# Giving the attention an accumulator bank of its own beside the second input projection

## The chip, the cores and the metric

The kernel runs on one core of one Trainium2 chip. The metric is the device time of one execution in microseconds; lower is better. A core has a matrix engine (TensorE, in the profile PE), VectorE (DVE), ScalarE (ACT), GpSimd (POOL) and SyncE (SP), which start transfers or compute side by side, each in its own fixed order. TensorE writes its results into eight accumulator banks of 512 single-precision columns; VectorE and ScalarE read them out.

## The reference, cut to what matters

One encoder layer runs over two sequences of 16 learned and 256 given positions (272 in all, width 1024), with shared weights.

```
h    = layer_norm(concat([meta, x]))
proj = h @ w_in                                   # z | xbc | dt | c_q | c_kv | k_rope
xbc  = silu(depthwise_conv(proj[xbc], conv_w))    # 5 taps; then the state-space scan in both directions
y_ssm  = rms_norm((y_f + y_b + d_skip * xs) * silu(z))
q      = rms_norm(c_q) @ w_uq ;  k_nope, v = rms_norm(c_kv) @ w_ukv
o      = softmax((q_nope k_nope^T + q_rope k_rope^T) / sqrt(96)) v       # 8 heads
y_attn = rms_norm(o)
h = layer_norm(alpha * h + concat([y_ssm, y_attn]) @ w_out)
h = layer_norm(alpha * h + peer_ffn(h))           # 8 heads choose 16 of 16384 experts each
```

## The kernel before

**Stages.** The first sequence is projected (`win(0)`), with its attention (`mla(0)`) mixed in. Then the second is projected (`win(1)`), while the first one's state-space scan (`ssd(0)`) and the second one's attention (`mla(1)`) are mixed in. After that come the first sequence's output projection (`wout(0)`) and expert queries, with the rest of `mla(1)` and `ssd(1)`, and at last the expert layer, which takes most of the time. The order of the last part is written out by hand (`manual_schedule`). In everything ahead of it a planner places each engine's instructions from the order of the program and its own estimate of when each can run; the chip then runs each engine's list as placed, and an instruction that has to wait holds up all behind it.

**Banks.** Each of the eight banks is a tile with one buffer. A new tile in a bank must wait until the last reader of the tile before it is done. `BANKS` gives, stage by stage, the banks of five users: the attention's scores and other small products (`at()`), the scan (`sa()`), the projection (`pm()`), the output projection (`wa()`), and the attention's products with weights (`mp()`). `phase(n)` sets them; a user takes its banks in turn, and starts a new turn only where its set has changed. In the first stage the projection has banks 0 to 2 and `mp()` has bank 7. In the second both have 0, 1 and 2, each with a turn of its own. In the third the projection has none and `mp()` has bank 2; in the fourth the projection has 0 and 1.

**The projection.** `win(s)` runs over 18 blocks of 128 channels and, in between, over four gate units of two tiles each, 26 accumulator tiles in all, in the order `W1`: 12, 8, 13, 9, 14, 15, 16, 17, 10, z0, 11, 0, z1, 1, 2, z2, 3, 4, z3, 5, 6, 7. A tile takes 24 matmuls (8 pieces of the width, each as three products of high and low parts, line 174). Weights are split into `whi` and `wlo` on ScalarE and VectorE (lines 151, 152), two of each in flight. What empties a tile depends on the block. Blocks 0 to 11 take one pass on ScalarE (line 433) and four convolution passes on VectorE (line 436), and line 440 then works without the bank. A gate tile takes a tanh (line 415) and a product (line 417). Blocks 13 to 17, the low-rank inputs of the attention, take a copy into `cn` (line 450) and a square into `sq` (line 452). `cn` has one buffer, so the second sequence's copies wait for the first attention's last read of it; `sq` has three, so blocks 16 and 17 must wait for the sums over the first three squares (line 459), which sit in a score bank.

**The attention.** `mla(1)` first computes scales: `Rk` is the copy of line 340, at the end of a chain of sums, a Newton root (`nrq`) and a broadcast (line 338). Then come eight key products (lines 355 and 356: two matmuls into a bank, then a product with `Rk` on VectorE that empties it), six value products (lines 363 and 364), and for each head a query product (line 370), read out as `qT` (lines 372, 373). For each block of queries there follow scores (line 376), maximum and scale (378, 379), exponential `Pm` (382), transposes (385), a copy `PT` (387), and the product with the values (391). Line 167 multiplies the key, value and query products, and those of `W_out`.

```
    mix(w1, (sd0, RS), (mla1, RM1))
```

mixes per step of the projection 0.55 steps of the scan and 0.3 of the attention. The first key products come in the program behind the tiles of z0, and all key and value products before z1's second tile.

Of the kernel before, what the change touches and what calls it, by code (L numbers as in the profile page):

```python
# [46 lines left out]
EROWS, MRATE = 4, 0.8  # L47
HP = 400
RM, RS2, RM3, RS3, Q0 = 0.6, 0.6, 1.0, 0.7, 13
BANKS = (((3, 4, 5, 6), (), (0, 1, 2), (), (7,)), ((3, 4, 5), (6, 7), (0, 1, 2), (), (0, 1, 2)),  # L50
         ((3, 4, 5), (6, 7), (), (0, 1), (2,)), ((3, 4, 5), (6, 7), (0, 1), (), (2,)),
         ((3, 4), (6, 7), (2, 5), (0, 1), ()), ((3, 4, 5), (6, 7), (0, 1, 2), (), ()))
DEL = (3, 2)
# [9 lines left out]
def build(ctx, tc, i, o):  # L63
# [189 lines left out]
    def phase(n):  # L253
        for k, b in enumerate(BANKS[n]):
            if b != held.get(k):
                held[k] = b
                sets[k] = banks(*b)
# [1133 lines left out]
```

## Time and profile before

| | |
|---|---|
| median of 3 runs | 1744.48 us |
| lowest and highest | 1744.19 and 1745.67 us |
| the profiled execution, its own time | 1745.9 us |
| its span in the profile | 1743.9 us |
| TensorE busy | 1678.4 us (96%) |
| VectorE busy | 1384.8 us (79%) |
| ScalarE busy | 683.4 us (39%) |
| GpSimd busy | 427.9 us (25%) |
| mean granted clock of TensorE | 0.978 |

The profile is one execution. Its span is 2.0 us shorter than the time that was measured for it. Busy time is the time in which an engine had an instruction under way; times below count from the span's start. The granted clock is a share of TensorE's full clock.

### The profile page before, as it was taken

The page shows a single profiled execution, that of the slowest core. Times are in us where ns is not written, and L with a number is a line of the kernel's source. Part 1 is how long each engine was busy: PE and PEld are TensorE (multiplying, and loading weights), DVE is VectorE, ACT ScalarE, POOL GpSimd, SP SyncE. Part 2 cuts the span into 40 slices and gives each one's busy share as a digit, 9 for nine tenths or more (in the row PEclk, how much of TensorE's full clock was granted, in tenths as well). Part 3 has the DMA queues.
Part 4 walks back from the last instruction along what each step waited for, and adds up shares of the span by engine and source line. Part 5 has one row for each costly group of instructions (what it writes and reads, how often), then busy time and mean ns, then how long its engine had stood idle before and what let it go on. Part 6 is the DMA issues. An engine that isn't in the chain of part 4 may idle for free.

```text
span 1743.9 us, 25363 instructions
## 1 busy us (share of the span) xinstructions
PE 1678.4 (96%) x9276; PEld 1468.7 (84%) x9276; DVE 1384.8 (79%) x2862; ACT 683.4 (39%) x1211; POOL 427.9 (25%) x372
## 2 busy tenths in 40 slices
PE   6999889999899999999999999999999999999997
PEld 5889868667748999999999888888999999999875
DVE  7676578487537999999998578888878888888886
ACT  4455665245203224545444333333333333333332
POOL 0000143033100000111121122222555555445320
PEclk9899899999999999999999999999999999999998
DMA  6453255553434435888899989999998999998872
GB/s 253 142 196 131 67 146 175 172 173 111 136 132 166 149 133 175 265 287 266 290 316 319 387 325 348 344 377 339 397 353 318 353 347 317 355 341 298 311 301 85
DMA packets 178349, 440.20 MB, mean 252 GB/s; under 512 B 13569, under 2 KB 87745, under 8 KB 174129
## 3 DMA queue, kind: packets, MB, share of 16 engines
q1 hardware_dynamic: 88336, 259.40, 41.9%
q0 software_dynamic: 37616, 137.83, 22.1%
q10 hardware_dynamic: 52272, 41.36, 7.4%
q8 instruction: 73, 1.20, 0.3%
q14 instruction: 52, 0.42, 0.1%
HBM read 392.33 MB, written 46.20 MB: 251 GB/s over the span
## 4 chain that ended last, share of the span: by engine, by line
PE 85%; DVE 6%; DMA 4%; ACT 3%; issue 1%; ACTq 0%; SPq 0%; DVEq 0%
PE bank L174 66%; PE bank L167 12%; DMA R<-rd 2%; DMA vraw<-in_v 2%; PE bank L915 1%; PE bank L916 1%; PE bank L391 1%; PE bank L376 1%; ACT whi L151 1%; DVE wlo L152 1%; DVE vlo L1116 1%; DMA mln_in_g<-in_ln_in_g 0%; PE bank L625 0%; DVE cv L436 0%; PE bank L385 0%
## 5 line engine op out<-in xcount | busy, mean ns | idle before, releaser
L174 PE MATMUL bank<-vhi,wh 128*128 128x512 f32 x756 | 296.6, 392 | 6.9 <-ACT wh L1115 6.9
L174 PE MATMUL bank<-vlo,wh 128*128 128x512 f32 x756 | 297.6, 394 | 0.7 <-DVE vlo L1116 0.6
L174 PE MATMUL bank<-vhi,wl 128*128 128x512 f32 x756 | 297.5, 394 | 0.0
L1008 POOL DMA_INDIRECT grow<-in_u,eidx x128 | 154.9, 1210 | 529.2 <-DVE grow L1026 480.3
L174 PE MATMUL bank<-x1T_hi,whi 128*128 128x384 f32 x832 | 283.2, 340 | 0.0
L174 PE MATMUL bank<-x1T_hi,wlo 128*128 128x384 f32 x832 | 279.1, 335 | 0.6 <-DVE wlo L1069 0.6
L174 PE MATMUL bank<-x1T_lo,whi 128*128 128x384 f32 x832 | 278.6, 335 | 0.0
L1116 DVE TENSOR_TENSOR vlo<-vraw,vhi 128x1024 fp32r<-128x1024 f32 x126 | 154.3, 1225 | 128.7 <-ACT vhi L1111 126.5
L1084 ACT ACTIVATE blk<-bank 128x384 f32<-128x384 f32 x128 | 62.9, 492 | 441.1 <-PE bank L174 441.1
L1008 POOL DMA_INDIRECT grow<-in_v,eidx x128 | 181.7, 1420 | 180.6 <-DVE x1g L1028 154.7
L1111 ACT CAST vhi<-vraw 128x1024 fp32r<-128x1024 f32 x126 | 131.9, 1047 | 193.1 <-issue 96.2
L174 PEld LDWEIGHTS bank<-vhi,wh 128*128 128x128 f32 x756 | 143.3, 190 | 36.8 <-ACT wh L1115 8.5
L174 PEld LDWEIGHTS bank<-vlo,wh 128*128 128x128 f32 x756 | 143.2, 189 | 30.9 <-DVE vlo L1116 2.0
L174 PEld LDWEIGHTS bank<-vhi,wl 128*128 128x128 f32 x756 | 143.1, 189 | 30.9 <-DVE wl L1117 0.8
L1028 DVE SCALAR_TENSOR_TENSOR x1g<-grow,act,x1g 128x1024 f32<-128x1024 f32 x128 | 164.0, 1281 | 4.5 <-DMA grow<-in_v,eidx 3.1
L174 PEld LDWEIGHTS bank<-x1T_lo,whi 128*128 128x128 f32 x832 | 156.3, 188 | 2.1
L174 PEld LDWEIGHTS bank<-x1T_hi,whi 128*128 128x128 f32 x832 | 156.3, 188 | 2.1
L174 PEld LDWEIGHTS bank<-x1T_hi,wlo 128*128 128x128 f32 x832 | 156.1, 188 | 0.9 <-DVE wlo L1069 0.9
L1026 DVE SCALAR_TENSOR_TENSOR grow<-grow,x1g 128x1024 f32<-128x1024 f32 x128 | 155.1, 1219 | 1.6 <-DMA grow<-in_u,eidx 1.4
L1069 DVE TENSOR_TENSOR wlo<-wraw,whi 128x1024 fp32r<-128x1024 f32 x104 | 126.8, 1219 | 14.9 <-ACT whi L1063 14.9
L1063 ACT CAST whi<-wraw 128x1024 fp32r<-128x1024 f32 x104 | 109.3, 1051 | 9.1 <-ACT stg L918 2.9
L174 PE MATMUL bank<-hT,whi 128*128 128x272 f32 x288 | 88.9, 309 | 5.0 <-DVE cv L520 3.4
(356 smaller groups left out, 3219.3 us busy)
## 6 DMA issues: line engine op xcount, KB each, us to landing
wraw<-in_uT SPq DMA_DIRECT2D x128, 512.0 KB
vraw<-in_v SPq DMA_DIRECT2D x128, 512.0 KB
gd<-stg ACTq DMA_DIRECT2D x24, 1024.0 KB
stg<-gd SPq DMA_DIRECT2D x15, 1536.0 KB
wraw<-in_w_in SPq DMA_DIRECT2D x36, 512.0 KB
hdr<-blk ACTq DMA_DIRECT2D x8, 1536.0 KB
blk<-hdr SPq DMA_DIRECT2D x8, 1536.0 KB
qraw<-in_w_q SPq DMA_DIRECT2D x19, 512.0 KB
```

Source lines behind the costliest of these rows:

```text
L151: nc.scalar.copy(hi[:, :n], raw[:, :n])
L152: lo_eng.tensor_tensor(lo[:, :n], raw[:, :n], hi[:, :n], op=OP.subtract)
L167: nc.tensor.matmul(out, a, b, start=(n == 0), stop=(n == n_all - 1))
L174: nc.tensor.matmul(out, a, b, start=(n == 0), stop=(n == n_all - 1))
L1008: nc.gpsimd.indirect_dma_start(out=rows[n], out_offset=None, in_=i["uv"[n // 128]], in_offset=bass.IndirectOffsetOnAxis(ap=eidx[:, n % 128 ...
L1026: nc.vector.scalar_tensor_tensor(r, r, 1.0, x1g, op0=OP.mult, op1=OP.mult, accum_out=act[:, k:k + 1])
L1028: nc.vector.scalar_tensor_tensor(x1g, r, act[:, k:k + 1], x1g, op0=OP.mult, op1=OP.add)
L1063: nc.scalar.copy(hi, ur[c])
L1069: nc.vector.tensor_tensor(lo, ur.pop(c), uw[c][0], op=OP.subtract)
L1084: nc.scalar.activation(hblk[c // 8][:, c % 8], pu, AF.Gelu)
L1111: nc.scalar.copy(hi, raw)
L1116: nc.vector.tensor_tensor(lo, raw, hi, op=OP.subtract)
```

## The change

In the second stage the projection keeps banks 0 and 1, and the attention's products with weights get bank 2 alone. The sets of the other stages stay. Since the projection's set differs from that of the first stage now, its turn starts anew at bank 0, where before it went on from the first stage's.

```
-BANKS = (((3, 4, 5, 6), (), (0, 1, 2), (), (7,)), ((3, 4, 5), (6, 7), (0, 1, 2), (), (0, 1, 2)),
+BANKS = (((3, 4, 5, 6), (), (0, 1, 2), (), (7,)), ((3, 4, 5), (6, 7), (0, 1), (), (2,)),
          ((3, 4, 5), (6, 7), (), (0, 1), (2,)), ((3, 4, 5), (6, 7), (0, 1), (), (2,)),
          ((3, 4), (6, 7), (2, 5), (0, 1), ()), ((3, 4, 5), (6, 7), (0, 1, 2), (), ()))
```

## Rows read from the trace of the kernel before

**Rows 1.** The page's first line, and the engines' shares of the chain.

```profile
span 1743.9 us, 25363 instructions
...
PE 85%; DVE 6%; DMA 4%; ACT 3%; issue 1%; ACTq 0%; SPq 0%; DVEq 0%
```

**Rows 2.** Busy time by stretch of the span; the first row names the columns.

```profile
core 0: us, PE busy (x) PEld busy (x) DVE busy (x) ACT busy (x) POOL busy (x), PEclk, DMA share, GB/s
...
171.00:181.00 10.00, 10.00 (x67) 9.03 (x66) 5.30 (x16) 6.74 (x19) 0.41 (x4) 1.00 0.40 125
...
199.30:204.50 5.20, 0.00 (x0) 0.00 (x0) 5.04 (x12) 3.09 (x4) 0.00 (x0) 0.64 0.11 40
204.50:217.70 13.20, 13.17 (x75) 12.52 (x76) 4.74 (x36) 5.70 (x16) 0.23 (x2) 0.63 0.01 2
...
221.00:265.00 44.00, 37.51 (x191) 26.76 (x189) 35.84 (x79) 26.48 (x72) 22.28 (x17) 0.92 0.57 171
...
250.00:265.00 15.00, 11.56 (x45) 6.83 (x45) 15.00 (x32) 10.47 (x32) 8.66 (x7) 0.89 0.52 175
265.00:325.00 60.00, 59.64 (x409) 52.24 (x408) 50.64 (x122) 30.70 (x64) 12.62 (x11) 1.00 0.56 177
...
340.00:380.00 40.00, 39.95 (x166) 23.56 (x165) 27.00 (x76) 18.49 (x57) 9.91 (x12) 1.00 0.44 143
```

**Rows 3.** The same view for line 174 alone: PE, PEld, clock, DMA.

```profile
171.00:180.90 9.90, 0.10 (x2) 0.01 (x1) 1.00 0.40 126
...
265.00:325.00 60.00, 40.50 (x288) 36.74 (x288) 1.00 0.56 177
...
317.20:320.70 3.50, 3.38 (x24) 3.14 (x24) 1.00 0.54 212
212.40:217.70 5.30, 5.29 (x25) 5.30 (x26) 0.50 0.01 2
```

**Rows 4.** Order of time on TensorE: start, length, instruction; idle time before it, releaser.

```profile
204.53 2.18 PE L167 MATMUL bank<-cn,araw 128*128 128x272 f32 x4 [5.27 <-DVE cv L436]
206.50 1.36 PE L385 MATMUL bank<-mats,Pm 128*96 128x128 f32 x6
...
232.14 0.49 PE L174 MATMUL bank<-hT,whi 128*128 128x272 f32 x1
...
263.78 1.19 PE L167 MATMUL bank<-cn,araw 128*128 128x272 f32 x4 [1.40 <-DVE cv L417]
...
267.34 0.36 PE L174 MATMUL bank<-whi,hT 128*128 128x256 f32 x1
...
281.85 0.28 PE L174 MATMUL bank<-whi,hT 128*128 128x256 f32 x1
...
284.12 0.65 PE L167 MATMUL bank<-cn,araw 128*128 128x256 f32 x2
...
306.85 0.37 PE L174 MATMUL bank<-hT,whi 128*128 128x272 f32 x1
```

**Rows 5.** Order of time on ScalarE.

```profile
180.06 0.49 ACT L450 ACTIVATE cn<-bank,chans 128x272 f32<-128x272 f32 x1 [1.04 <-PE bank L167]
...
205.07 0.20 ACT L382 ACTIVATION_READ_ACCUMULATOR Pm<-bank,mx,scr 128x1 f32 x1
...
208.68 0.69 ACT L452 ACTIVATE sq<-bank 128x272 f32<-128x272 f32 x2 [0.26 <-PE bank L459]
...
229.38 0.38 ACT L340 COPY sq<-bank 64x272 f32<-64x272 f32 x1
```

**Rows 6.** VectorE: order of time, groups of 195 to 205 us, line 440's lengths.

```profile
203.74 0.20 DVE L379 TENSOR_SCALAR mx<-mx,scr 128x1 f32<-128x1 f32 x1
...
282.35 1.56 DVE L436 SCALAR_TENSOR_TENSOR cv<-bank,chans,cv 128x271 f32<-128x271 f32 x3
...
309.39 0.41 DVE L417 SCALAR_TENSOR_TENSOR cv<-th,bank 128x256 f32<-128x256 f32 x1
...
L436 DVE SCALAR_TENSOR_TENSOR cv<-bank,chans,cv 128x270 f32<-128x270 f32 (+1 forms) x4 | 2.0, 497 | 0.1
...
L440 DVE SCALAR_TENSOR_TENSOR blk<-th,cv x12: 431/435/4157, 219.8 to 324.4; 128x272 f32<-128x272 f32 x12
```

## The prediction

> **What bounds the kernel now.** The page says that TensorE's matmuls fill nearly the whole span: the chain that ended last is 85% TensorE, and the span is 1743.9 us [rows 1]. So an edit is worth what it takes from, or adds to, the time in which TensorE stands or runs slowly. The second projection's stage starts when the first sequence's attention is about to end, near 197 us, and its last projection tile is multiplied by 320.7 us. I read a table of stretches over it [rows 2], then the order of events on TensorE, ScalarE and VectorE at the places where that table shows losses [rows 3 to 6].
>
> Two places lose time. Between 199.3 and 204.5 us TensorE does nothing, and from 204.5 to 217.7 us its granted clock averages 0.63; between the two levels, 0.50 stands for 1.2 GHz and 1.00 for 2.4 GHz [rows 2]. What ends the idle time is named: a key product of the second sequence (line 167) waited 5.27 us for a convolution pass on VectorE [rows 4]. That pass reads an accumulator of the projection, because `pm()` and `mp()` share banks 0 to 2. The second loss is from 221 to 265 us: TensorE is busy 37.51 of 44.00 us, so 6.5 us are idle, and the clock averages 0.92 [rows 2]. There the sharing works the other way. A key product can only be read out once `Rk` is there, and the copy that makes `Rk` starts at 229.38 us [rows 5]. The key product of 204.53 us sits in its bank until then, two more follow into the other banks, and behind them the next projection tile (channel block 11) starts at 232.14 us [rows 4]. Later, another key product waits 1.40 us for a gate's pass at 263.78 us, and the second tile of z1, queued in its bank behind the last value product, starts only at 267.34 us [rows 4].
>
> From 265 to 325 us TensorE is busy 59.64 of 60.00 us, and from 340 to 380 us 39.95 of 40.00 [rows 2]. Time won before 265 us therefore moves everything behind it forward, if VectorE follows. That is the doubt: VectorE is busy all 15.00 us of 250 to 265, and 50.64 us of the 60 after it [rows 2].
>
> **The change, part by part.** No instruction is added or removed; the same 26 projection tiles, 14 key and value products and 2 query products of the stage go to other banks. But nothing before the last part is ordered by hand: the planner places each engine's instructions anew, so the sum is of waits, not of operations.
>
> (a) *The wait of 5.27 us goes.* Bank 2 is free early, so the first key product can run while the attention drains. What is late next? The transposes of the attention's weights (line 385) start at 206.50 us, right behind the key product; their input is the exponential whose last piece starts at 205.07 us and lasts 0.20 [rows 4, 5]. Alone, then, 1.2 us are won. More is won because of (b): block 10 no longer reaches VectorE in this drain. Its passes take 497 ns each, and three of the four begin before the step at 203.74 us on which the exponential waits [rows 6]: 1.5 us. Together 2.7 us. The upper bound counts all four passes, 1.2 + 2.0 = 3.2 us; the lower is 1.2.
>
> (b) *Block 10 moves behind the drain.* With two banks in strict turn, blocks 16 and 17 hold both of them until their squares are taken on ScalarE, at 208.68 us [rows 5]. Before, block 10 had the third bank and was multiplied ahead of the idle stretch. Earlier too a tile is lost: blocks 13, 14 and 16 sat in the three banks until the first attention's last query product let the `cn` tile go, at 180.06 us [rows 5]; with two banks it is one tile fewer. One tile of 24 matmuls costs 3.4 us at the full clock and 25 matmuls cost 5.29 us at the low one [rows 3]. If the place that it leaves stays idle, up to 5.1 us are lost; if the attention moves up into it, nothing. From 171 to 181 us the attention alone, with hardly a projection matmul in it, kept TensorE busy 10.00 of 10.00 us [rows 2, 3], so I stay near nothing: 1.0 us lost.
>
> (c) *The projection no longer waits for `Rk`.* Blocks 11, 0 and the z1 tiles can follow as soon as their own banks are read out. At stake are 6.5 us of idle time and, by the clock, 0.08 of 37.51 us, 3.0 us: 9.5 us in all [rows 2]. The lower bound is 0, since VectorE is full from 250 to 265 us and two tiles more would want passes there. It has 21 us of work in the 29 before that (35.84 less 15.00 [rows 2]), so part fits. I take half, 4.7 us. The key and value products now go one at a time through bank 2; they are not late, for the first query product comes only at 284.12 us [rows 4].
>
> (d) *Two banks instead of three from 265 us on.* I laid each tile's first matmul beside the end of the pass that empties the tile two before it, as if nothing else moved. Six tiles would be late: z2's first tile starts at 281.85 us while block 1 is read until 282.35 + 1.56 = 283.91 us, so 2.1 us; block 5 starts at 306.85 us while z3's first tile is read until 309.39 + 0.41 = 309.80 us, so 3.0 us [rows 4, 6]. The others are 0.6, 1.2, 4.9 and 0.6 us; the sum is 12.4 us. That is the upper bound, nothing the lower. Of the 59.64 us, 40.50 are projection [rows 2, 3]; the other 19.1 us (state-space, attention, then `W_out`) are there to be put into such holes. They are more than 12.4, so I stay near nothing: 2.0 us lost.
>
> Sum: 2.7 - 1.0 + 4.7 - 2.0 = 4.4 us won. The profiled execution took 1745.9 us, 2.0 more than its span, and becomes 1741.5; it lies 1.4 above the median of 1744.48, so on the median's footing the forecast is 1740.1 us. All bounds in favour (3.2 + 9.5) give 1731.8; all against (1.2 - 5.1 - 12.4) give 1760.8.
>
> The Trainium skill speaks against (d): "Perfetto Trace Analysis", section Optimizing Tensor Performance, Matmuls, wants independent groups of matmuls to rotate through banks, so that one is read out while the next is multiplied. Here the projection's rotation shrinks to two and the key products lose theirs. If that rule decides, it is the third case below.
>
> **The rivals.** *VectorE is the bound.* The passes cannot be done sooner, and what TensorE gains in (c) it waits for later: c is 0, and 2.7 - 1.0 - 2.0 leaves 0.3 us lost, 1744.8. For it: 15.00 of 15.00 us, and a gated product at line 440 that took up to 4157 ns where its median is 435 [rows 2, 6]. Against it: VectorE is busy 27.00 of 40.00 us from 340 to 380, so deferred work has room [rows 2]. A new order in which the planner undoes the gain elsewhere lands here too.
>
> *Two banks bite.* The projection waits for convolution passes behind the six tiles of (d), in an order of TensorE's queue in which nothing stands ready behind the waiting matmul; nothing comes of (c). Half of 12.4 us gives 2.7 - 1.0 - 6.2 = 4.5 us lost, 1749.0; all of it gives 1755.2. It decides from 1.7 us on if (c) gives nothing, from 6.4 us on if (c) gives its 4.7. For it: the six late tiles. Against: the 19.1 us of other work.
>
> *All of it comes back.* 1731.8 us as above. Against it: VectorE again.
>
> *The sharing was harmless.* The drain is held by the attention's own chain (exponential, transposes, squares), and key products only filled it: then (a) is at its 1.2 us, (b) costs its 1.0, and the rest is as in the first rival. It is counted with it.
>
> **How the numbers follow.** Forecast (gain of some 3.5 to 10 us): 0.43; all of it: 0.07; VectorE bound or harmless: 0.28; two banks bite: 0.22. About 0.2%, 3.5 us, is what can be told from no change here. So faster 0.50, same 0.28, slower 0.22. The range reaches from 1731.5 to 1750, past the half price of the third case and short of its full one; the likeliest case's own range is 1734 to 1741.
>
> **What the profile after would show.** For (a): no idle stretch of 5 us ended by a convolution pass in front of line 167 near 200 us, and transposes before 206. For (b): block 10's convolution after the squares. For (c): block 11 starts before the copy that makes `Rk` or close to it, and less than 3 us of idle time in the 45 us behind z0. For (d): waits of line 174 for lines 436 or 417; under 3 us in all is right, over 6 wrong. The prediction is wrong if the low clock returns in 221 to 265 us, or if the planner's new order costs elsewhere ahead of the hand-written last part.

## The result, and the profile after

| | before | after |
|---|---|---|
| median of 10 runs each | 1745.08 us | 1755.64 us |
| lowest and highest | 1737.6 and 1748.61 | 1750.45 and 1759.14 |
| span of the profiled execution | 1743.9 | 1754.6 |

The change made the kernel slower: ratio 1.0067, 95% interval 1.0051 to 1.0082. The forecast was 1740.1 us, and the time lies above its range. Three executions among the runs further below, of 2109.88, 4282.91 and 9274.0 us, the last being the profiled one of before_rs75, are slow ones and enter no ratio.

The changed kernel's page, first line, engine shares and chain, answering [rows 1]:

```profile
span 1754.6 us, 25358 instructions
...
PE 1681.9 (96%) x9276; PEld 1469.8 (84%) x9276; DVE 1385.1 (79%) x2862; ACT 682.7 (39%) x1211; POOL 426.3 (24%) x372
...
PE 86%; DVE 5%; DMA 4%; ACT 2%; issue 2%; POOL 0%; ACTq 0%; SPq 0%; DVEq 0%; POOLq 0%
```

**Where the time went.** Everything ahead of the hand-written part ends with the scaling of the second sequence's scan output (line 671), at 470.81 us before and 480.77 after. I cut the span there and at four milestones: 160 us, the reading of z0's second tile, the second projection's last convolution pass, and the last add of the first output projection. Busy time by these stretches, first of the kernel before, then of the changed one (columns as in [rows 2]):

```profile
0.00:160.00 160.00, 138.72 (x943) 128.92 (x944) 118.26 (x278) 73.61 (x134) 4.76 (x15) 0.95 0.56 190
160.00:224.66 64.66, 58.33 (x392) 53.04 (x391) 37.54 (x111) 40.19 (x100) 6.59 (x19) 0.89 0.21 66
224.66:323.82 99.16, 92.98 (x583) 77.33 (x583) 81.68 (x187) 53.83 (x127) 34.73 (x28) 0.97 0.57 177
323.82:384.41 60.59, 60.54 (x243) 35.23 (x242) 33.54 (x101) 24.25 (x73) 12.10 (x16) 1.00 0.47 155
384.41:470.81 86.40, 78.50 (x409) 64.65 (x407) 57.67 (x240) 38.18 (x108) 26.39 (x28) 0.94 0.37 121
0.00:470.81 470.81, 429.06 (x2563) 359.18 (x2563) 328.69 (x914) 230.06 (x540) 84.58 (x105) 0.95 0.46 153
470.81:1743.90 1273.09, 1249.33 (x6715) 1109.48 (x6714) 1056.10 (x1948) 453.32 (x671) 343.30 (x267) 0.99 0.81 289
```

```profile
0.00:160.00 160.00, 138.28 (x931) 128.05 (x932) 117.74 (x278) 72.31 (x134) 4.36 (x15) 0.95 0.55 187
160.00:225.74 65.74, 58.91 (x404) 53.29 (x403) 37.59 (x113) 40.37 (x102) 6.62 (x18) 0.94 0.24 75
225.74:328.68 102.94, 97.00 (x612) 83.03 (x611) 80.05 (x178) 56.34 (x133) 34.62 (x30) 0.94 0.55 173
328.68:383.56 54.88, 53.36 (x195) 28.35 (x194) 31.49 (x100) 18.26 (x54) 8.07 (x9) 1.00 0.41 132
383.56:480.77 97.21, 85.06 (x429) 68.18 (x427) 61.77 (x248) 42.35 (x118) 30.65 (x33) 0.91 0.37 124
0.00:480.77 480.77, 432.61 (x2563) 360.91 (x2563) 328.64 (x914) 229.62 (x540) 84.32 (x105) 0.94 0.45 150
480.77:1754.60 1273.83, 1249.34 (x6715) 1108.93 (x6714) 1056.43 (x1948) 453.10 (x671) 342.01 (x267) 0.99 0.81 289
```

The hand-written part takes 1273.09 and 1273.83 us. Of the 10.7 us of span, 9.96 lie ahead of it, on the same 2563 matmul records. There TensorE idles 480.77 - 432.61 = 48.16 us against 41.75, and is busy 3.55 us longer for the same work, which the mean clock (0.94 against 0.95) goes with. By stretch the idle time changes by +0.44, +0.50, -0.24, +1.47 and +4.25 us: most of it arises after the second projection, where no bank was reassigned. The clock changes by some -0.1, -1.0, +2.0, 0.0 and +2.3 us by stretch; this is an estimate, TensorE's busy time weighted by one minus the clock granted during it.

**What the drain and the stage show.** Five rows of stretches answer [rows 2]:

```profile
199.30:204.50 5.20, 5.07 (x27) 4.65 (x28) 1.36 (x3) 3.36 (x10) 0.11 (x1) 0.64 0.25 76
204.50:217.70 13.20, 11.75 (x88) 11.37 (x88) 6.51 (x39) 4.71 (x12) 0.11 (x1) 0.88 0.16 52
221.00:265.00 44.00, 35.76 (x183) 27.36 (x184) 32.34 (x72) 23.58 (x60) 17.60 (x13) 0.85 0.44 135
250.00:265.00 15.00, 10.89 (x53) 8.33 (x54) 11.58 (x31) 10.95 (x30) 6.49 (x5) 0.79 0.44 137
265.00:325.00 60.00, 60.00 (x420) 54.39 (x419) 50.35 (x111) 33.88 (x77) 17.02 (x18) 1.00 0.61 195
```

The hole of 5.20 us is filled, and 204.5 to 217.7 us runs at 0.88 where it was 0.63. But 221 to 265 us got worse: 8.24 us idle for 6.49, clock 0.85 for 0.92. VectorE, full from 250 to 265 us before, is busy 11.58 of 15.00.

The waits of TensorE from 160 to 340 us, grouped (us in total, times, longest), before and after:

```profile
PE bank L167 <- DVE cv L436: 5.3, 1, 5.3
PE bank L572 <- DVE y L641: 1.7, 1, 1.7
PE bank L167 <- DVE cv L417: 1.4, 1, 1.4
...
PE bank L167 <- DVE kT L356: 0.9, 2, 0.6
...
```

```profile
PE bank L167 <- DVE kT L356: 3.9, 2, 3.6
PE bank L572 <- DVE blk L235: 2.5, 1, 2.5
PE bank L174 <- DVE wlo L152: 1.7, 2, 1.0
PE bank L391 <- ACT PT L387: 1.6, 2, 1.4
PE bank L625 <- POOL A L622: 0.9, 1, 0.9
...
```

Both waits for the projection's passes (5.3 and 1.4) are gone, and others of the same size took their place: all groups of the two lists add up to 12.3 and 12.6 us. The new longest wait, 3.6 us, comes with the change in this order; with the own bank and another turn of the scores' or the scan's banks (after_at453, after_at534, after_sa76 below) the longest such wait is 0.4 us, 1.6 us and none. In order of time on TensorE, and below it on VectorE:

```profile
203.17 1.49 PE L385 MATMUL bank<-mats,Pm 128*96 128x128 f32 x6
...
226.94 0.60 PE L174 MATMUL bank<-hT,whi 128*128 128x272 f32 x1
...
260.58 2.18 PE L167 MATMUL bank<-cn,araw 128*128 128x272 f32 x4 [3.63 <-DVE kT L356]
```

```profile
251.64 0.42 DVE L356 TENSOR_TENSOR kT<-bank,sq 64x272 f32<-64x272 f32 x1
...
257.66 0.29 DVE L616 TENSOR_SCALAR A<-R,cs 128x128 f32<-128x128 f32 x1 [3.27 <-DMA R<-rd]
...
260.10 0.43 DVE L356 TENSOR_TENSOR kT<-bank,sq 64x272 f32<-64x272 f32 x1
```

A key product is read out on VectorE at 260.10 us, late because VectorE stands 3.27 us on a scan transfer (R) placed ahead of it and then works off the scan. With one bank the next key product can't start until that is done, and TensorE's list has it in front.

### The profile page after: what moved, and what is told of

The parts are those of the page before. It is cut to its first block, busy times and chain, and to the rows that moved or that the text cites. A ratio compares the mean times of both kernels' runs of the same rounds, so it can differ in the third digit from the quotient of the medians.

```text
span 1754.6 us, 25358 instructions
## 1 busy us (share of the span) xinstructions
PE 1681.9 (96%) x9276; PEld 1469.8 (84%) x9276; DVE 1385.1 (79%) x2862; ACT 682.7 (39%) x1211; POOL 426.3 (24%) x372
## 4 chain that ended last, share of the span: by engine, by line
PE 86%; DVE 5%; DMA 4%; ACT 2%; issue 2%; POOL 0%; ACTq 0%; SPq 0%; DVEq 0%; POOLq 0%
PE bank L174 66%; PE bank L167 12%; DMA R<-rd 2%; PE bank L915 1%; PE bank L916 1%; PE bank L391 1%; DMA vraw<-in_v 1%; PE bank L376 1%; DMA mln_in_g<-in_ln_in_g 1%; DVE wlo L152 0%; DVE A L616 0%; PE bank L385 0%; PE bank L625 0%; PE bank L801 0%; DVE Dm L618 0%
```

## The experiments

The theories. *Own bank*: the change costs by itself (key and value products go one at a time, K in the expectations, or two banks hold up the projection, T). *Late scan* (S): the freed projection runs ahead, the first scan falls behind (its last product on line 655 begins at 298.64 us for 288.25), and that lateness is paid for at the end. *The planner's order* (P): any edit makes the planner place everything anew, and the orders differ by more than the sharing does. Of each diff only the second stage's sets stand here: scores, scan, projection, output, products with weights.

**The parts, and a turn as control.** ctl_turn keeps the sharing and begins both turns at bank 1. proj_two takes the third bank from the projection alone; attn_one gives the products bank 2 alone while the projection keeps three; after_rs75 changes the changed kernel's scan rate.

```
-((3, 4, 5), (6, 7), (0, 1, 2), (), (0, 1, 2))
+((3, 4, 5), (6, 7), (1, 2, 0), (), (1, 2, 0))    ctl_turn
+((3, 4, 5), (6, 7), (0, 1), (), (0, 1, 2))       proj_two
+((3, 4, 5), (6, 7), (0, 1, 2), (), (2,))         attn_one
-R0, RS, RM1 = 1.05, 0.55, 0.3
+R0, RS, RM1 = 1.05, 0.75, 0.3                    after_rs75
```

> A control for the planner's scatter: the kernel before with the second stage's two users still sharing all three banks, only the turn rotated (1, 2, 0), so that other tiles meet in a bank. Theory S (the freed projection runs ahead of the first sequence's scan, and the scan's lateness is paid after 384 us), theory K (one bank makes the key and value products serial, so the attention is late) and theory T (two banks make the projection wait for convolution passes): no change, 1741 to 1749 us. Theory P (any new order of the planner costs some 10 us): 1750 us or more, or 1740 or less.

> Half the change: the projection keeps banks 0 and 1, the attention's products still go round 0, 1 and 2. Theory T: most of the loss is there, 1752 us or more, with waits of line 174 for lines 436 or 417. Theory K: no change, 1741 to 1749. Theory S: key products again sit in the projection's banks until Rk, so the projection is held back and the scan is not overtaken: 1741 to 1749, last product of the first scan by 292 us.

> The other half: the projection keeps three banks, the attention's products are confined to bank 2, which they share with it. Theory K: most of the loss is there, 1752 us or more, with the values late (last value copy near 290 us in place of 274). Theory T: no change. Theory S: two banks of the projection are free of key products, so it runs ahead as in the changed kernel and the first scan ends 5 to 10 us late: 1749 to 1756.

> The changed kernel, with the first scan mixed in at 0.75 steps for each step of the projection in place of 0.55, so that it stands earlier in the program. Theory S: the scan's last product comes before 292 us in place of 298.6, and 5 to 12 us come back: 1744 to 1751 us. Theories K and T: the banks are as in the changed kernel, so the time is too: 1753 to 1758. Theory P: anything.

Measured, as ratios to before: ctl_turn 1.0081 (1.0052 to 1.0110), proj_two 1.0105 (1.0070 to 1.0140), attn_one 1.0202 (1.0171 to 1.0232), after_rs75 1.0043 (1.0026 to 1.0061). The control, which moves no bank from one user to the other, costs as much as the change. Each part alone costs more than both together, so the parts don't add up. Both came out slow as K and T said of them: in attn_one the last value copy starts at 294.04 us, while in proj_two the waits of line 174 for line 436 come to only 1.9 us. The higher scan rate won some 4 us over the change by the ratios, whose intervals overlap (6 by the medians). That spoke for the late scan, though the first scan's last product still began at 294.52 us and not before 292.

**The change under other numbers, the sharing under another turn.**

```
-((3, 4, 5), (6, 7), (0, 1, 2), (), (0, 1, 2))
+((3, 4, 5), (6, 7), (0, 2), (), (1,))            own_02_1
+((3, 4, 5), (6, 7), (1, 2), (), (0,))            own_12_0
+((3, 4, 5), (6, 7), (1, 0), (), (2,))            own_10_2
+((3, 4, 5), (6, 7), (2, 0, 1), (), (2, 0, 1))    shr_201
```

> The change with other bank numbers: in the second stage the projection has 0 and 2, the attention's products bank 1. Nothing computed differs. Theory 'a bank of its own costs by itself' (one bank makes the key and value products serial, two make the projection wait): like the change, 1751 to 1760 us, ratio 1.004 to 1.009. Theory 'the planner's order decides and the sharing matters little': anywhere from 1740 to 1765; a time under 1748 or over 1763 in any of the three own-bank variants speaks for it.

> The change with other bank numbers: the projection has 1 and 2, the attention's products bank 0. Theory 'own bank costs by itself': 1751 to 1760 us. Theory 'the planner's order decides': 1740 to 1765, and not where the other two are.

> The change with its turn begun at the other bank: the projection has 1 and 0, the attention's products bank 2. It is the smallest step from the change that a planner can be given. Theory 'own bank costs by itself': 1752 to 1759 us. Theory 'the planner's order decides': more than 4 us from the change to either side is likely.

> The sharing of before, three banks for both, but both turns begin at bank 2. Theory 'own bank costs by itself': 1742 to 1748 us, like before, and the neutral rotation run earlier was the exception. Theory 'the planner's order decides': 1740 to 1765, most likely slower than before by over 4 us, as the other rotation was (1.0081), since before is then a favourable order.

Measured: own_02_1 1.0073 (1.0051 to 1.0095), own_12_0 1.0069 (1.0046 to 1.0092), own_10_2 1.0021 (1.0004 to 1.0039), shr_201 1.0050 (1.0031 to 1.0070). The first two came out as "own bank costs by itself" said, the last two did not. own_10_2 is the change with its projection turn begun at bank 1 instead of 0: 1745.98 us, some 8 less than the change by its ratio. It keeps the new long wait (first group of its waits from 160 to 340 us), and its part ahead of the hand-written one ends at 472.35 us:

```profile
PE bank L167 <- DVE kT L356: 4.4, 2, 4.1
```

```profile
0.00:472.35 472.35, 425.75 (x2563) 354.95 (x2563) 335.20 (x914) 230.92 (x540) 83.38 (x105) 0.96 0.46 153
```

It stands longer there than the change (4.4 against 3.9 us) and is still 8.4 us ahead of it at the end of that part (480.77), so that wait doesn't decide the total. Most of the difference is busy time: 46.60 us idle against the change's 48.16, but 425.75 busy against 432.61 for the same 2563 records, at a clock of 0.96 against 0.94.

**Edits that touch neither user, and the scan's rate on both sides.** before_at453 and after_at453 begin the scores' turn at bank 4, in the kernel before and in the changed one. before_rs75 and own102_rs75 take the scan rate of 0.75 to the kernel before and to own_10_2.

```
-((3, 4, 5), (6, 7), (0, 1, 2), (), (0, 1, 2))
+((4, 5, 3), (6, 7), (0, 1, 2), (), (0, 1, 2))    before_at453
-((3, 4, 5), (6, 7), (0, 1), (), (2,))
+((4, 5, 3), (6, 7), (0, 1), (), (2,))            after_at453
```

> The kernel before with the turn of the score banks in the second stage begun at 4 (4, 5, 3 for 3, 4, 5); projection and products with weights share banks 0 to 2 as before. Nothing that the change touches is touched. Theory 'any new order of the planner costs some us, before is a favourable one': 1747 to 1762 us, ratio 1.002 to 1.010. Theory 'who shares the projection's banks decides': 1742 to 1747 us, no difference.

> The changed kernel with the turn of the score banks in the second stage begun at 4. Theory 'the planner's order decides': more than 4 us from the change's 1755.6 to either side, within 1742 to 1765. Theory 'own bank costs by itself': 1753 to 1759 us.

> The kernel before with 0.75 instead of 0.55 steps of the scan mixed in per step of the second projection. In the changed kernel this won 6 us (the first scan ended 4 us sooner). Theory 'the change makes the projection run ahead of the scan, and the scan's lateness is what is paid for': before has no such lateness (its scan ended 10 us sooner), so within 3 us of before, 1741 to 1748. Theory 'the planner's order decides': another throw, 1745 to 1760.

> Own bank with the projection's turn begun at bank 1 (1745.98 us), and 0.75 instead of 0.55 steps of the scan per step of the projection. Theory 'the scan's lateness is paid for': 1739 to 1744 us, since its first scan still ends 5 us later than that of before. Theory 'the planner's order decides': 1743 to 1758, since 1746 was already among the good orders.

Measured: before_at453 1.0079 (1.0051 to 1.0108), after_at453 1.0039 (1.0017 to 1.0061), before_rs75 1.0040 (1.0016 to 1.0063), own102_rs75 1.0051 (1.0030 to 1.0073). before_at453 has the shared banks and the same two waits that the change was to remove, and yet costs about as much as the change. Its waits from 160 to 340 us, and its part ahead of the hand-written one:

```profile
PE bank L167 <- DVE cv L436: 5.3, 1, 5.3
PE bank L174 <- DVE wlo L152: 3.6, 3, 1.8
PE bank L338 <- DVE dg L337: 1.6, 2, 0.8
PE bank L167 <- DVE cv L417: 1.3, 1, 1.3
...
```

```profile
0.00:483.22 483.22, 435.76 (x2563) 365.64 (x2563) 327.86 (x914) 231.46 (x540) 80.31 (x105) 0.94 0.45 149
```

The late scan falls as the cause. In ctl_turn, shr_201 and before_at453 the first scan's last product begins at 286.62, 285.52 and 285.30 us, earlier than before's 288.25, and all three are slow; in own_10_2 it begins at 293.27 us, and that kernel is nearly as fast as before. The runs with the higher rate don't decide it: own102_rs75 is slower than own_10_2, but its scan's product didn't come sooner (295.22 us), and where that of before_rs75 came isn't known. That after_rs75 won is then no evidence for the late scan.

**Two more pairs.** A price of the sharing of some 5 us could still hide in the scatter, so two neutral edits were made on both kernels: the scores' turn at bank 5, and the scan's banks in the order 7, 6.

```
-((3, 4, 5), (6, 7), ...
+((5, 3, 4), (6, 7), ...    before_at534, after_at534
+((3, 4, 5), (7, 6), ...    before_sa76, after_sa76
```

> The kernel before with the turn of the score banks in the second stage begun at 5. Projection and products with weights share as before. Theory 'the loss is the planner's new order, and the sharing has no price of its own': 1746 to 1762 us, a neutral edit again slower than before. Theory 'sharing is better by itself by some 5 us, and the score turn at 4 was an unlucky exception': 1742 to 1748.

> The changed kernel with the same neutral edit, a pair with the run before it. Theory 'no price of its own': 1742 to 1762, above or below its partner with like chance. Theory 'sharing is better by itself': 5 us or more above its partner.

> The kernel before with the scan's two banks in the second stage taken in the order 7, 6. Theory 'no price of its own': 1746 to 1762 us. Theory 'sharing is better by itself': 1742 to 1748.

> The changed kernel with the scan's banks in the order 7, 6, a pair with the run before it. Theory 'no price of its own': 1742 to 1762 us, above or below its partner; over all pairs (unedited, score turn at 4, at 5, scan turn, projection turn) the mean difference stays within 5 us of nothing. Theory 'sharing is better by itself': 5 us or more above its partner, as the unedited pair is (12.6).

Measured: before_at534 1.0140 (1.0109 to 1.0170), after_at534 1.0170 (1.0140 to 1.0201), before_sa76 1.0001 (0.9984 to 1.0017), after_sa76 1.0053 (1.0035 to 1.0072). Both runs with the turn at 5 lie above every range that was expected of them, and the pair with the scan's banks came out as "sharing is better by itself" said. All pairs of one edit with and without the sharing (ctl_turn turns the products' banks too, of which own_10_2 has only one):

| edit on both sides | banks shared | own bank | own less shared |
|---|---|---|---|
| none | 1 (before) | 1.0067 (after) | +0.67% |
| projection's turn begun at bank 1 | 1.0081 (ctl_turn) | 1.0021 (own_10_2) | -0.60% |
| scores' turn at 4 | 1.0079 | 1.0039 | -0.40% |
| scores' turn at 5 | 1.0140 | 1.0170 | +0.30% |
| scan's turn 7, 6 | 1.0001 | 1.0053 | +0.52% |
| scan rate 0.75 | 1.0040 | 1.0043 | +0.03% |

The mean difference is +0.09%, with a standard deviation of 0.51 and so a standard error of 0.21: 1.5 us, give or take 3.6. With six pairs anything between a gain of some 8 us and a price of some 11 can't be excluded (2.57 standard errors). What is excluded is a steady price of 0.67%: in two pairs the own bank is the faster one, by 0.60 and 0.40%. Unpaired, at the scan rate of 0.55, the seven kernels with an own bank (own_02_1 and own_12_0 among them) average 1.0070, and the six with the banks shared as before 1.0059.

With the sharing kept, five edits that leave alone who uses which banks (ctl_turn, shr_201, before_at453, before_at534, before_sa76) gave 1.0081, 1.0050, 1.0079, 1.0140 and 1.0001, on average 1.0070. Before is one of the two fastest of these six orders, and a new order costs on average what the change cost; why before is so well placed isn't known. That these edits do make new orders is seen in the traces: TensorE's list parts from that of before after 784 matmuls in the changed kernel (at 137.5 us of before's span), and after 784, 1470, 1230, 1230 and 1130 in the five. The differences lie ahead of the hand-written part, which takes between 1267.25 and 1273.9 us in all profiled kernels here but before_rs75, while the planned part ends at 470.81 us in before, 473.33 in before_sa76, 494.16 in before_at534 and 502.51 in attn_one. proj_two (1.0105) lies inside that scatter and says nothing of its part; attn_one (1.0202) lies outside it, the only one of the sharing kind that does, and what costs it so much was not followed up.

## Why the prediction was wrong

**The drain, (a) and (b): right in kind, smaller in size.** The wait of 5.27 us is gone, the transposes start at 203.17 us (before 206, as said), and block 10 is read by its first convolution pass only at 212.26 us, behind the squares at 201.55 us (ScalarE in order of time). From 160 us to z0's reading, 0.5 us more of idle time against some 1.0 less at the low clock leave 0.5 us won, where 2.7 - 1.0 = 1.7 was forecast. What came late next was not the transposes alone: lines 572 and 391 waited 2.5 and 1.6 us for the attention's last steps.

**(c) failed.** Block 11 starts at 226.94 us for 232.14 [rows 4], but the copy that makes `Rk` also came sooner, at 224.06 us for 229.38 [rows 5], so the block still starts 2.9 us behind it. In the 45 us behind z0, TensorE is busy 39.06 us (39.18 before), so 5.94 are idle where under 3 was the mark, and the low clock came back (0.85 from 221 to 265 us). VectorE, the doubt of the first rival, was not full there: 32.34 of 44.00 us. My bound for (c), nothing lost at worst, looked at the projection alone: the sharing's other side is that three banks let key products run ahead of their reading, and one doesn't. In this order that wait (3.6 us) and those for weight pieces and the scan took the place of the old ones.

**(d) was right for this order.** No group of the list from 160 to 340 us has line 174 waiting for 436 or 417, and from 265 to 325 us TensorE is busy 60.00 of 60.00. The Trainium skill's rule in "Perfetto Trace Analysis", section Optimizing Tensor Performance, Matmuls, on rotating through banks had no bite on the projection's two banks here; on the key products, whose rotation is gone, the trace agrees with it (0.9 us of waits for line 356 became 3.9). Both depend on the order. In after_at534, with the same two banks and the one, a projection tile waits 5.3 us for a convolution pass, and the key products wait 1.6:

```profile
PE bank L174 <- DVE cv L436: 5.7, 2, 5.3
...
PE bank L167 <- DVE kT L356: 1.6, 1, 1.6
...
```

So that nothing waits doesn't show that two banks are free of cost: the planner can have put other work where the projection would have waited. (c) and (d) together gave 1.8 us lost (idle -0.2, clock +2.0, by unrounded sums) for 2.7 won.

**The step that failed most** is the sentence that time won before 265 us "therefore moves everything behind it forward, if VectorE follows". A full TensorE from 265 to 325 us does not carry a gain onward; it shows that the planner had enough work to put there, whichever work it was. In the changed kernel the second tile of z1 is read 9.95 us sooner (264.53 for 274.48 us on VectorE) and the last value copy starts 17 us later (290.66 for 273.42 on ScalarE); first before, then after:

```profile
273.42 0.46 ACT L364 ACTIVATE V<-bank,rs 96x256 f32<-96x256 f32 x1
274.48 0.41 DVE L417 SCALAR_TENSOR_TENSOR cv<-th,bank 128x256 f32<-128x256 f32 x1
```

```profile
264.53 0.40 DVE L417 SCALAR_TENSOR_TENSOR cv<-th,bank 128x256 f32<-128x256 f32 x1
290.66 0.47 ACT L364 ACTIVATE V<-bank,rs 80x256 f32<-80x256 f32 x1 [0.52 <-PE bank L167]
```

What ran ahead had pushed something else back, and the sum of the stage's waits told nothing of the end. The loss came after it: 1.5 us in the output projection and 6.5 behind it. TensorE's waits from the last add of the output projection to the end of the planned part, which add up to 7.8 us before and 12.1 after, begin:

```profile
PE bank L234 <- ACT ob L401: 4.9, 1, 4.9
PE bank L167 <- DVE qT L373: 2.4, 2, 1.4
PE bank L376 <- ACT ob L393: 0.5, 1, 0.5
```

```profile
PE bank L234 <- ACT ob L401: 4.9, 1, 4.9
PE bank L586 <- ACT A L615: 2.2, 1, 2.2
PE bank L646 <- DVE nr L188: 2.1, 1, 2.1
PE bank L572 <- ACT cb L574: 1.1, 1, 1.1
PE bank L167 <- DVE qT L373: 0.6, 1, 0.6
...
```

The new ones belong to the second sequence's scan (lines 572, 586, 646). That these are late because of this order is read from the trace, not tried by itself.

In the span's terms, 4.4 won was forecast and 10.7 lost, 15.1 apart: 1.2 in (a) and (b), 4.5 in (c) and (d), and 8.3 in stretches for which the sum had no term at all (0.3 ahead of 160 us, 1.5 in the output projection, 6.5 behind it). The rest, some 1.1, is the 0.7 of the hand-written part and 0.4 that this count doesn't place. The rival "two banks bite" ends near the measured time, 1755.2, but is not what happened. The prediction named the true danger, a new order that costs elsewhere, and priced it in the first rival at 0.3 us lost. The five neutral edits put it at 0 to 1.4%.

**What stays open:** which of the planner's decisions costs the time, and whether the own bank has a price or gain of its own within the bounds above. An order held fixed while only the banks change would settle the second; it was not tried.

## What to carry to other kernels

Where a planner orders the work, an edit's first effect is a new order, and its scatter is the yardstick: time a few edits that change nothing of substance (begin a turn of banks elsewhere) before giving a difference a cause, and compare the edit in pairs under several of them. A stall that disappears from a full stage is no gain until the last milestone of the planned part moves; follow the idle time and the clock to that point. Before taking a buffer from a sharer, see who runs ahead by means of it: in the changed kernel's order it was the key products.

## What was not expected of the hardware

One order of instructions takes different times in different executions by more than the waits argued about here. In the hand-written part of before and of own_10_2, with 6715 matmul records in each, TensorE's, VectorE's and ScalarE's lists are the same, and it took 1273.09 us in the one profile and 1267.25 in the other:

```profile
472.35:1739.60 1267.25, 1245.98 (x6715) 1106.99 (x6714) 1056.54 (x1948) 453.23 (x672) 341.81 (x267) 0.99 0.82 290
```

So that kernel's profiled span, 4.3 us below that of before, is not a gain: over all its runs the ratio to before is 1.0021.
